# Neighbourhood attention in slots of two units, with scores over row halves of the array

## The chip, the cores and the metric

The kernel runs on one core of one Trainium2 chip. The core has a matrix engine (TensorE, in the profile PE for its matmuls and PEld for its weight loads), a vector engine (VectorE, DVE), a scalar engine (ScalarE, ACT), a general engine (GpSimd, POOL) and a sync engine (SyncE, SP) that mainly issues transfers. Each engine has its own list of instructions, in the order of the program, and waits on semaphores for what the others produce. The metric is the device time of one execution, in microseconds; smaller is better.

## What is computed

The reference is one layer of a bidirectional hybrid encoder over 2048 tokens of width 1024, seen as a grid of 32 rows and 64 columns. One projection yields the inputs of eight attention heads (64 wide) and of four mLSTM heads (128 wide); both branches are gated, concatenated, projected back and added to the input, and a last RMSNorm follows. The change concerns the attention: every token attends to a window of 8 rows and 16 columns.

```python
def neighbourhood_attention(q, k, v, rpb):
    ...
    qg = to_grid(q) * (NA_HEAD_DIM ** -0.5)
    kgrid, vgrid = to_grid(k), to_grid(v)
    ...
    s = jnp.einsum('bhrcd,bhrjkd->bhrcjk', qg, kg).astype(jnp.float32) + bias[None]
    s = jnp.where(col_mask[:, None, :], s, -jnp.inf)
    p = jax.nn.softmax(s.reshape(B, NA_HEADS, rows, GRID_W, kh * GRID_W), axis=-1).reshape(s.shape)
    o = jnp.einsum('bhrcjk,bhrjkd->bhrcd', p, vg)
    ...
def hybrid_mixer(...):
    na_out = neighbourhood_attention(na_q, na_k, na_v, rpb) * jax.nn.silu(na_z)
    ...
    return jnp.concatenate([na_out, ml_out], axis=-1) @ w_out
...
h_res = h_res + gate[:, None, :] * y
return rmsnorm(h_res, final_norm_w).astype(x.dtype)
```

## The kernel before

**Precision.** Large products are made in a one-pass format (F32R) from operands that are split into a high part and a low part, x = hi + lo. A product is the sum of three: hi by hi, hi by lo, lo by hi. The low part is made by ScalarE writing hi and VectorE (or POOL) subtracting it from x.

**Stages.** Phase 1 normalises the input and projects the mLSTM branch. Phase 1b (lines 931 to 962) runs the mLSTM recurrence head by head, and fills the gaps of TensorE with the remaining projections, which `nq_gen` (line 844) yields matmul by matmul: the gates of both branches, then k, then q. The function `pump(n)` (line 917) takes n steps of that stream, and later of the output projections. Phase 2 (line 1209) is attention with the output projection as the filling.

**Keys.** k is kept on chip in four tiles `kk[ct]`, one for two heads (64 rows each). They lie in the memory that the normalised input of token groups 3 and 2 held. The upper half of k goes out to memory and is read back by `kk_jobs` (line 976), sixteen transfers, one at every second step of the recurrence; the lower half is written straight from PSUM (lines 879 to 888). For head j of the pair, a column range of `kk[ct]` holds the high part in 64 rows and the low part in the other 64.

**Queries.** For two units, q is loaded into `qhigh` (the high part twice, in both halves of the rows) and `qlow` (the low part, in the 64 rows of its head, zeros elsewhere, set once by POOL). A matmul with `qhigh` over all 128 rows makes hi by hi plus hi by lo at once, one with `qlow` makes lo by hi. From the fourth load on, `double_q` (line 1267) makes the second copy on VectorE.

**Units and slots.** The grid is cut into 16 patches of 8 by 16 tokens (128 queries). A patch sees 264 to 480 keys. A unit is a patch and two heads, 64 units in all. A slot (line 1531) works on three units at a time:

- `stage_s(n)`: scores, two matmuls a head (lines 1353 and 1354), into a PSUM tile of the pool pS (three buffers); then for each head VectorE adds the bias table and takes the row minimum (line 1359; the scores are negated), ScalarE takes exp with the row sum (line 1360), and the table of a later unit is loaded over the one just used.
- `stage_o(n-2)`: probabilities by v (line 1396), with 64 output columns a head, so each matmul uses half of the array's columns; then VectorE multiplies by the gate (line 1398).
- `stage_t(n-1)`: PE transposes of the normalised probabilities into pT (two buffers, line 1381), evicted by ScalarE (line 1383) into two tiles `pt`.
- `stage_n(n)`: VectorE takes the reciprocal of the sums and normalises (lines 1369 and 1371).
- When a patch is done, its gated output (and the mLSTM half) is split: `mix_high` on ScalarE (line 1406), `mix_low` on VectorE (line 1411). `outproj` (line 1413) is the generator of its 48 projection matmuls (two halves of the output columns, eight blocks of channels, three products each), followed by the addition to x (line 1440), the sum of squares on ScalarE (line 1442), and the scale and the store as later small steps.
- At last, `pump(22)` in the first four slots, all that is left of the q projections in slot 4, and `pump(12)` after that.

In the entry (slots 0 to 5) the stream still holds the last q projections. The dictionary `first` (line 1497) says in which slot which loads and which splits of the output weights (`split_w`, line 1333: ScalarE line 1334, VectorE line 1335) are issued. `load_v`, `load_z` and `load_q(2)` of the first patch stand before slot 0 (lines 1525 to 1527), on POOL's queue.

Phase 2's slots are issued under a manual schedule: the order of the program is the order on each engine.

Of the kernel before, what the change touches and what calls it, by code (L numbers as in the profile page):

```python
# [62 lines left out]
class Kernel:  # L63
# [780 lines left out]
    def nq_gen(self):  # L844
# [10 lines left out]
        for i, s, g in order:  # L855
# [23 lines left out]
            if kind == "k" and g in lower:  # L879

                for j in range(2):
                    rows, other = slice(j * HD, (j + 1) * HD), slice((1 - j) * HD, (2 - j) * HD)
                    cols = slice(j * T + g * GT, j * T + (g + 1) * GT)
                    hv = self.kk[ct][rows, cols]
                    nc.scalar.activation(hv, ps[rows], AF.Identity, bias=bias[rows])
                    nc.vector.scalar_tensor_tensor(self.kk[ct][other, cols], ps[rows], bias[rows], hv.bitcast(F32), ALU.add, ALU.subtract)
                yield
                continue
# [87 lines left out]
    def kk_jobs(self):  # L976

        flat = lambda t: t.rearrange("p a b -> p (a b)")
        self.kk = [flat(t) for g in (3, 2) for t in (self.hhi[g], self.hlo[g])]

        def load(ct, j, hl):
            src = self.d_kna[hl, ct * P + j * HD : ct * P + (j + 1) * HD, T // 2 :]
            row = j * HD if hl == 0 else (1 - j) * HD
            self.nc.sync.dma_start(self.kk[ct][row : row + HD, j * T + T // 2 : (j + 1) * T].bitcast(F32), src)

        return [[((3, 2)[ct // 2], lambda a=(ct, j, hl): load(*a)) for j in range(2) for hl in range(2)] for ct in range(4)]
# [67 lines left out]
    def ml_pass2(self, ml, h):  # L1054
# [11 lines left out]
        def load_z(gi):  # L1066
            while ("mz", h, gi) not in self.zdone:
                self.pump(1)
            if h == MH - 1 and gi == NG - 1:
                t = self.p2.tile([P, 4, P], F32, tag="pt", bufs=2, name="zt_last")  # L1070
# [138 lines left out]
    def phase2(self):  # L1209
# [29 lines left out]
        qhigh = [p.tile([P, 2, 2, P], F32R, name=f"qhigh{i}") for i in range(3)]  # L1239
        qlow = [p.tile([P, 2, 2, P], F32R, name=f"qlow{i}") for i in range(3)]  # L1240
# [14 lines left out]
        def load_q(i):  # L1255
# [3 lines left out]
            hi, lo = qhigh[i % 3], qlow[i % 3]  # L1259
            src = self.d_qna[0, c0 // 2, b].rearrange("(j p) c q -> p j c q", j=2)  # L1260
            for rows in (slice(0, HD), slice(HD, P))[: 2 if i < 3 else 1]:
                (nc.gpsimd if i < 3 else nc.sync).dma_start(hi[rows].bitcast(F32), src)
            for j in range(2):
                js = slice(j * HD, (j + 1) * HD)
                (nc.gpsimd if i < 3 else nc.sync).dma_start(lo[js, j].bitcast(F32), self.d_qna[1, c0 // 2, b, js])

        def double_q(i):
            hi = qhigh[i % 3]
            nc.vector.tensor_copy(hi[HD:], hi[:HD].bitcast(F32))
# [70 lines left out]
        def stage_s(u):  # L1340
            b, ct = units[u]
            pr, pc, nr, nkc, nk, rpc, nch = geo[b]
            at, c = (u // 2) % 3, ct % 2
            pts = []
            sums = few.tile([P, 2], F32, tag="sums", bufs=3, name=f"sums_{u}")
            scores = []
            rs = slice(PR_R0[pr], PR_R0[pr] + nr)
            cs = slice(PC_C0[pc], PC_C0[pc] + nkc)
            for j in range(2):
                ps = pS.tile([P, 512], F32, tag="pS", name=f"pS_{u}_{j}")[:, :nk]  # L1350
                kv = kk[ct][:, j * T : (j + 1) * T].rearrange("p (r c) -> p r c", c=GRID_W)[:, rs, cs]
                o = ps.rearrange("p (r c) -> p r c", c=nkc)
                nc.tensor.matmul(o, qhigh[at][:, j, c, :], kv, start=True, stop=False)  # L1353
                nc.tensor.matmul(o, qlow[at][:, j, c, :], kv, start=False, stop=True)  # L1354
                scores.append(ps)
            for j, ps in enumerate(scores):
# [5 lines left out]
                if u in follows:  # L1362
                    load_tab(follows[u], j)
# [290 lines left out]
```

## Time and profile before

| what | value |
|---|---|
| median of 3 runs | 1388.04 us (1387.38 to 1388.36) |
| the profiled execution, its own time | 1394.31 us |
| its span in the trace | 1392.3 us |
| mean granted clock of TensorE | 0.985 |
| first score of attention (unit 0) | 1014.2 us after the start of the span |
| last value matmuls | 1362.3 us |
| idle TensorE from 1010 to 1030 us | 1.87 us |
| idle TensorE from 1100 to 1363 us | 0 us |

The page of the profile gives busy times for each engine, the chain of work that ended last, and the costliest groups of instructions. A timeline row gives the start in microseconds from the start of the span, the duration, the engine, the line of the kernel, the operation, what is written and read, the shape, and, in brackets, the idle time before it with what ended it. Matmuls are pipelined: a row's duration reaches over the start of the next, so what one costs is the distance from start to start. Rows with x2 or more are several instructions merged.

### The profile page before, as it was taken

How to read it: one execution, taken by the hardware profiler on the slowest of the kernel's cores; microseconds unless marked ns; L12 is line 12 of the kernel's file. 1: busy time of each engine (PE TensorE's matmuls, PEld its weight loads, DVE VectorE, ACT ScalarE, POOL GpSimd, SP SyncE). 2: the span in 40 equal slices, each digit the busy share in tenths (PEclk: the TensorE clock that was granted, in tenths of full speed). 3: DMA queues.
4: the chain of work that ended last, by engine and by line, in shares of the span. 5: the costliest groups of instructions: out<-in, count | busy, mean ns of one | idle time of the engine just before them, and what ended most of it. 6: DMA issues, size and time to landing. Idle time of an engine off the chain costs nothing.

```text
span 1392.3 us, 23366 instructions
## 1 busy us (share of the span) xinstructions
PE 1307.3 (94%) x8076; PEld 1124.4 (81%) x8076; DVE 823.7 (59%) x2497; ACT 528.7 (38%) x1131; POOL 293.7 (21%) x323
## 2 busy tenths in 40 slices
PE   2989999997999899999999999799998999999996
PEld 2989998987877787888878787688876888888885
DVE  6683323211255559156867777877636776777673
ACT  4642334523233323112323313233335555555551
POOL 4453222424101010001212002112402211111121
PEclk9999999999999999999999999999999999999999
DMA  9799439778458685565766888846687896876872
GB/s 317 224 288 226 121 108 230 187 193 192 135 111 216 145 186 159 170 168 146 201 191 204 247 233 226 211 131 185 177 242 232 188 226 162 198 196 169 190 182 61
DMA packets 269723, 263.68 MB, mean 189 GB/s; under 512 B 33482, under 2 KB 230090, under 8 KB 269606
## 3 DMA queue, kind: packets, MB, share of 16 engines
q1 hardware_dynamic: 178062, 186.45, 50.3%
q0 software_dynamic: 21520, 37.73, 11.0%
q10 hardware_dynamic: 70024, 38.02, 9.7%
q8 instruction: 64, 1.05, 0.3%
q14 instruction: 53, 0.43, 0.1%
HBM read 177.57 MB, written 92.72 MB: 194 GB/s over the span
## 4 chain that ended last, share of the span: by engine, by line
PE 51%; DMA 6%; DVE 4%; issue 3%; ACT 1%; POOL 1%; SPq 0%; ACTq 0%; POOLq 0%; DVEq 0%
PE pq L865 17%; PE y L1435 13%; PE pO L1396 4%; PE pT L1381 4%; DMA kv<-d_ck 3%; PE pc L430 2%; PE pc L431 2%; PE pc L429 2%; PE pS L1353 2%; PE px L1091 2%; PE pi L1093 2%; PE pS L1354 2%; PE dc L1039 1%; DMA d_qna<-qst 1%; PE a L1078 1%
## 5 line engine op out<-in xcount | busy, mean ns | idle before, releaser
L865 PE MATMUL pq<-hhi,whi_a 128*128 128x512 f32 x512 | 208.3, 407 | 2.1 <-ACT whi_a L841 1.3
L865 PE MATMUL pq<-hhi,wlo_a 128*128 128x512 f32 x512 | 208.2, 407 | 0.5 <-DVE wlo_a L842 0.5
L865 PE MATMUL pq<-hlo,whi_a 128*128 128x512 f32 x512 | 208.6, 407 | 0.0
L1360 ACT ACTIVATE pbuf<-pbuf,mn 128x480 f32<-128x480 f32 (+5 forms) x128 | 76.3, 597 | 103.3 <-DVE mn L1359 103.1
L865 PEld LDWEIGHTS pq<-hhi,whi_a 128*128 128x128 f32 x512 | 97.4, 190 | 20.1 <-ACT whi_a L841 1.8
L865 PEld LDWEIGHTS pq<-hhi,wlo_a 128*128 128x128 f32 x512 | 97.3, 190 | 17.8 <-DVE wlo_a L842 1.0
L865 PEld LDWEIGHTS pq<-hlo,whi_a 128*128 128x128 f32 x512 | 97.1, 190 | 16.5
L1435 PE MATMUL y<-hhi,whi_a 128*128 128x512 f32 x256 | 86.1, 405 | 3.1 <-ACT hhi L1334 2.8
L1435 PE MATMUL y<-hhi,wlo_a 128*128 128x512 f32 (+1 forms) x272 | 85.1, 386 | 0.2 <-ACT y L1442 0.2
L1359 DVE CUSTOM_DVE_ANT_0 pbuf<-pS,tab 128x480 f32<-128x480 f32 (+5 forms) x128 | 65.1, 541 | 32.6 <-PE pS L1354 24.2
L839 POOL TENSOR_TENSOR wlo_a<-rawq,whi_a 128x1024 fp32r<-128x1024 f32 x20 | 48.1, 2406 | 165.9 <-ACT whi_a L838 124.2
L1115 POOL TENSOR_TENSOR hm<-hm,ck 128x128 f32<-128x128 f32 x64 | 26.3, 412 | 264.1 <-DVE hm L1114 188.8
L429 PE MATMUL pvo<-whi_b,hhi 128*128 128x256 f32 x256 | 74.8, 292 | 5.3 <-DVE stvo L499 5.3
L1096 ACT ACTIVATE num<-px,gtile 128x129 f32<-128x129 f32 x120 | 38.2, 365 | 99.5 <-PE px L1091 83.5
L1023 DVE TENSOR_SCALAR wv<-kv,gtile 128x129 f32<-128x129 f32 x120 | 39.1, 333 | 60.9 <-DMA kv<-d_ck 31.9
L430 PE MATMUL pvo<-wlo_b,hhi 128*128 128x256 f32 x256 | 73.6, 287 | 0.0
L431 PE MATMUL pvo<-whi_b,hlo 128*128 128x256 f32 x256 | 73.5, 287 | 0.0
L714 ACT ACTIVATE dec<-dec,gtile 128x128 f32<-128x128 f32 x128 | 42.1, 392 | 72.3 <-POOL dec L710 63.4
L499 DVE TENSOR_TENSOR stvo<-pvo,brow 128x256 f32<-128x256 f32 x64 | 26.5, 420 | 70.0 <-PE pvo L431 56.2
L464 DVE TENSOR_TENSOR stv<-pv,brow 128x256 f32<-128x256 f32 x32 | 12.4, 421 | 90.2 <-DMA d_vna<-stv 49.1
L1396 PE MATMUL pO<-pt,v 128*64 128x128 f32 (+3 forms) x832 | 60.8, 282 | 0.0
L1381 PE MATMUL pT<-ident,pbuf 128*128 128x128 f32 (+2 forms) x416 | 59.1, 280 | 0.0
(302 smaller groups left out, 3573.0 us busy)
## 6 DMA issues: line engine op xcount, KB each, us to landing
ck<-d_ck SPq DMA_DIRECT2D x64, 384.5 KB
kv<-d_ck SPq DMA_DIRECT2D x120, 128.5 KB
rawq<-in_w_main_dram SPq DMA_DIRECT2D x28, 512.0 KB
raw<-in_w_main_dram SPq DMA_DIRECT2D x20, 512.0 KB
d_ck<-stvo SPq DMA_DIRECT2D x16, 514.0 KB
x<-in_x_dram SPq DMA_DIRECT2D x16, 512.0 KB
wada<-in_w_ada_dram SPq DMA_DIRECT2D x32, 256.0 KB
dec<-d_mneg SPq DMA_DIRECT2D x32, 256.0 KB
```

The costliest lines, as they stand in the source:

```text
L429: nc.tensor.matmul(ps, lhi(k), rhi(k), start=(k == 0), stop=False)
L430: nc.tensor.matmul(ps, lhi(k), rlo(k), start=False, stop=False)
L431: nc.tensor.matmul(ps, llo(k), rhi(k), start=False, stop=(k == KT - 1))
L714: nc.scalar.activation(t[:, d, o, :], t[:, d, o, :], AF.Exp, bias=self.cols["g"][:, d, h, c : c + 1])
L839: nc.gpsimd.tensor_tensor(lo[:, :, cs], raw, hi[:, :, cs].bitcast(F32), ALU.subtract)
L865: nc.tensor.matmul(patch_ps(ps) if patch else ps, w, self.htok(h, g, k, patch), start=(k == 0 and n == 0), stop=(k == KT - 1 and n == 2))
L1023: nc.vector.tensor_scalar(wv, tiles[d, i][:, 128:257], self.cols["w"][:, d, h, c : c + 1], None, ALU.mult)
L1359: nc.vector.tensor_tensor_reduce(pt[:, :nk], ps, tabs[place[u]][j][:, :nk], 1.0, 3e38, ALU.add, ALU.min, mn)
L1360: nc.scalar.activation(pt[:, :nk], pt[:, :nk], AF.Exp, bias=mn, scale=-1.0, accum_out=sums[:, j : j + 1])
L1381: nc.tensor.transpose(ps[:cs, i, :], pts[j][:, i * cs : (i + 1) * cs], self.ident)
L1396: nc.tensor.matmul(po[j * HD : (j + 1) * HD, :], v[:n, h * HD : (h + 1) * HD], pt[j][:n, i, :], start=(i == 0), stop=(i == nch - 1))
L1435: nc.tensor.matmul(y, m[:, k, :], w[k][:, cs], start=(k == 4 and n == 0), stop=(k == 3 and n == 2))
```

## The change

The change rewrites attention's slots and the layout of q and k that its scores read.

- **Layout.** `kk[ct]` holds the high part of both heads in its first T columns and the low part in the next T, with head j in rows 64j to 64j+63. `kk_jobs` has eight transfers of 128 rows where it had sixteen of 64, at the same pace. The lower half's eviction is one ScalarE and one VectorE instruction over 128 rows where it was two and two over 64. q is one tile `qs` of high and low parts, loaded by one transfer; the zeros, the second copy and `double_q` go.
- **Scores.** `scores(pair)` makes for each unit three matmuls a head over the 64 rows of that head, the two heads in turn: high by high, low by high, high by low. pS has four buffers.
- **Slots of two units.** Slot m makes the scores of units 2m and 2m+1, the value matmuls of the two units before (one PSUM tile, one gating instruction), normalises the new pair, and transposes it within the same slot: four times one head's transposes into the single buffer of pT, each followed by its eviction into one of four `pt` tiles and by some steps of the projection stream. The steps of a slot are 44 in the first two and 24 after that.
- **What stands behind the evictions.** The sum of squares (`self.squares`) is no longer issued when the projection ends but behind the next eviction; so are the splits of a finished patch, and the weight splits, one to an eviction. The dictionary `extra` gives their places. The first patch's v, z and q loads are issued in slot 0.

```diff
             if kind == "k" and g in lower:
-                for j in range(2):
-                    rows, other = slice(j * HD, (j + 1) * HD), slice((1 - j) * HD, (2 - j) * HD)
-                    cols = slice(j * T + g * GT, j * T + (g + 1) * GT)
-                    hv = self.kk[ct][rows, cols]
-                    nc.scalar.activation(hv, ps[rows], AF.Identity, bias=bias[rows])
-                    nc.vector.scalar_tensor_tensor(self.kk[ct][other, cols], ps[rows], bias[rows], hv.bitcast(F32), ALU.add, ALU.subtract)
+                hv, lv = (self.kk[ct][:, e * T + g * GT : e * T + (g + 1) * GT] for e in range(2))
+                nc.scalar.activation(hv, ps, AF.Identity, bias=bias)
+                nc.vector.scalar_tensor_tensor(lv, ps, bias, hv.bitcast(F32), ALU.add, ALU.subtract)
...
-        def load(ct, j, hl):
-            src = self.d_kna[hl, ct * P + j * HD : ct * P + (j + 1) * HD, T // 2 :]
...
+        def load(ct, e):
+            src = self.d_kna[e, ct * P : (ct + 1) * P, T // 2 :]
+            self.nc.sync.dma_start(self.kk[ct][:, e * T + T // 2 : (e + 1) * T].bitcast(F32), src)
...
+            (nc.gpsimd if i < 3 else nc.sync).dma_start(qs[i % 3].bitcast(F32), self.d_qna[:, c0 // 2, b].rearrange("e p c q -> p e c q"))
-        def double_q(i):
...
+        def scores(pair):
...
+                for n, (e, f) in enumerate(((0, 0), (1, 0), (0, 1))):
+                    for j, ps in enumerate(made[u]):
+                        js = slice(j * HD, (j + 1) * HD)
+                        o = ps.rearrange("p (r c) -> p r c", c=nkc)
+                        nc.tensor.matmul(o, q[js, e, c, :], keys[f][js], start=(n == 0), stop=(n == 2))
...
+        def turned(u, j):
...
+            for i in range(nch):
+                nc.tensor.transpose(ps[:cs, i, :], U[u][j][:, i * cs : (i + 1) * cs], self.ident)
+            t = p.tile([P, 4, P], F32, tag="pt", bufs=4, name=f"pt_{u}_{j}")
+            nc.scalar.activation(t[:cs, :nch, :], ps[:cs, :nch, :], AF.Copy)
...
-                    nc.scalar.activation(y, x, AF.Square, accum_out=ssq[:, at : at + 1])
+                    square = lambda x=x, y=y, at=at: nc.scalar.activation(y, x, AF.Square, accum_out=ssq[:, at : at + 1])
+                    if end:
+                        square()
+                    else:
+                        self.squares.append(square)
...
-        pS = self.pool(pss, "pS", bufs=3, space=PSUM)
-        pT = self.pool(pss, "pT", bufs=2, space=PSUM)
+        pS = self.pool(pss, "pS", bufs=4, space=PSUM)
+        pT = self.pool(pss, "pT", bufs=1, space=PSUM)
...
+        extra = {
+            (0, -1): [lambda: load_v(b0), lambda: nc.sync.dma_start(zs[1], self.d_mix[b0])],
+            (0, 0): [lambda: load_z(b0), lambda: load_q(2)],
+            (1, 2): [lambda: load_w(4), lambda: load_w(5), lambda: load_w(6), lambda: load_w(7)],
+            (2, 0): [lambda: split_w(4)],
+            (2, 1): [lambda: load_z(b1), lambda: split_w(5)],
+            (2, 2): [lambda: split_w(6), lambda: load_x(b0)],
+            (2, 3): [lambda: split_w(7)],
...
+        def slot(m):
+            new = (2 * m, 2 * m + 1) if 2 * m < NU else ()
+            old = (2 * m - 2, 2 * m - 1) if m else ()
+            if m:
+                load_q(m + 2)
+            if new:
+                scores(new)
+            if old:
+                po = values(old)
+            if new:
+                normalised(new[0])
+            if old:
+                gated(old, po)
+            if new:
+                normalised(new[1])
...
+            fills = [10, 9, 9, 8, 8] if m < 2 else [6, 5, 5, 4, 4]
+            for fn in extra.pop((m, -1), ()):
+                fn()
+            self.pump(fills[0])
+            for n, (u, j) in enumerate([(u, j) for u in new for j in range(2)]):
+                turned(u, j)
+                if n % 2:
+                    step()
+                finish()
+                if n == 1:
+                    if m == 2:
+                        self.pump(max(0, self.left) + 1)
+                        self.owed = 0
+                    mixed(1)
+                if n == 2:
+                    mixed(0)
+                for fn in extra.pop((m, n), ()):
+                    fn()
+                self.pump(fills[n + 1])
```

196 lines of the change are left out of this document (79 added, 117 removed).

## The prediction

> **What bounds the kernel now.** I read the busy shares first, then the chain of waits, then busy time by stretch.
>
> ```profile
> PE 1307.3 (94%) x8076; PEld 1124.4 (81%) x8076; DVE 823.7 (59%) x2497; ACT 528.7 (38%) x1131; POOL 293.7 (21%) x323
> PE 51%; DMA 6%; DVE 4%; issue 3%; ACT 1%; POOL 1%; SPq 0%; ACTq 0%; POOLq 0%; DVEq 0%
> 1030.00:1060.00 30.00, 26.40 (x159) 20.34 (x157) 16.16 (x43) 14.94 (x33) 5.19 (x9) 0.96 0.96 303
> 1100.00:1200.00 100.00, 100.00 (x692) 81.52 (x691) 72.00 (x236) 53.55 (x144) 18.31 (x29) 1.00 0.83 191
> ```
>
> In a stretch the columns are its length, busy PE, PEld, DVE, ACT and POOL, the granted clock, DMA share and GB/s. Attention is bound by TensorE: it never rests from 1100 to 1200 us, while VectorE is 72% and ScalarE 54% busy. So a change there is worth what it takes off or adds to TensorE's own instructions, as long as nothing comes late to them. Only the entry (1030 to 1060 us) has idle TensorE, 3.6 us.
>
> One unit (two heads of a patch) looks like this, first with 384 keys, then the end of one with 480, then a score with 264:
>
> ```profile
> 1200.82 0.34 PE L1353 MATMUL pS<-hhi,qhigh 128*128 128x384 f32 x1
> 1201.00 0.34 PE L1354 MATMUL pS<-hhi,qlow 128*128 128x384 f32 x1
> 1201.62 0.88 PE L1396 MATMUL pO<-pt,v 128*64 128x128 f32 x12
> 1202.43 0.88 PE L1381 MATMUL pT<-ident,pbuf 128*128 128x128 f32 x6
> 1203.06 0.70 PE L1435 MATMUL y<-hhi,whi_a 128*128 128x512 f32 x2
> ...
> 1142.38 0.38 PE L1353 MATMUL pS<-hlo,qhigh 128*128 128x480 f32 x1
> 1142.60 0.38 PE L1354 MATMUL pS<-hlo,qlow 128*128 128x480 f32 x1
> 1142.92 1.09 PE L1396 MATMUL pO<-pt,v 128*64 128x128 f32 x16
> 1143.94 1.09 PE L1381 MATMUL pT<-ident,pbuf 128*128 128x128 f32 x8
> 1144.79 0.70 PE L1435 MATMUL y<-hhi,whi_a 128*128 128x512 f32 x2
> 1145.33 0.39 PE L1435 MATMUL y<-hlo,whi_a 128*128 128x512 f32 x1
> ...
> 1097.49 0.29 PE L1353 MATMUL pS<-hhi,qhigh 128*128 128x264 f32 x1
> 1097.61 0.28 PE L1354 MATMUL pS<-hhi,qlow 128*128 128x264 f32 x1
> ```
>
> Start to start is what an instruction costs. A score takes 0.12 us with 264 keys, 0.18 with 384, 0.22 with 480: 0.46 ns a key. The value stage takes 0.81 us for 12 matmuls and 1.02 for 16, so 0.0525 each and 0.18 fixed: the switch from half-array (128*64) matmuls back to whole ones. The switch into them is 1142.60 to 1142.92 less the 0.22, so 0.10. That is 0.28 a unit, 0.14 a switch. A transpose is 0.105 (0.63 for 6), and the output projection 0.23 (1145.33, less the two before it: 0.27 each, so the step from transposes to projection costs under 0.1).
>
> **The change, part by part.** The forecast adds these terms.
>
> *Scores.* Before, four matmuls a unit over all 128 rows. After, six over 64 rows, alternately rows 0-63 and 64-127, into different PSUM tiles. The patches have 264, 288, 360, 360 keys and 352, 384, 480, 480, each list twice: 5936 keys, by 4 units, by 4 matmuls, by 0.46 ns is 43.7 us now. If the two of a pair run side by side, it is 3/4 of that, 32.8: a gain of 10.9. If they run in turn, it is 6/4, 65.5: a loss of 21.8. Row halves are not in this trace. The nearest rows are the column halves of the value stage. Two such matmuls take 0.105, as one transpose of 128 columns does, and their weight loads end in pairs, as three cuts of one stage show:
>
> ```profile
> 1142.97 0.24 PEld L1396 LDWEIGHTS pO<-pt,v 128*64 128x64 f32 x3
> 1142.97 0.25 PEld L1396 LDWEIGHTS pO<-pt,v 128*64 128x64 f32 x4
> 1142.97 0.35 PEld L1396 LDWEIGHTS pO<-pt,v 128*64 128x64 f32 x5
> ```
>
> The fourth load ends 0.01 after the third, the fifth 0.10 later. So halves of the array load and multiply side by side, and I take -10.9.
>
> The Trainium skill, in "TensorE: Matmul & The Clock Gate" (LDWEIGHTS), lets a load's time go by its columns and not its rows, 128 columns at 1.2 GHz, so a 64-row load would cost a whole one, about 107 ns. By that, with loads in turn, the scores would be the third rival below; the paired ends above speak against it. The page's part on row tiling has matmuls in different row groups run at once, which no row here shows for rows.
>
> *Switches.* Before, two a unit: 128. After, three a pair of units (into row halves, to column halves, back): 96. At 0.14 that is -4.5. The new kinds could cost 0 or double (0 to 0.28 for two of three), so -13 to +4.5; I take -4.5, since all three end one shape and begin another. Transposes now come in four bursts a pair instead of two; a burst inside a run of projections costs nothing extra:
>
> ```profile
> 989.42 0.38 PE L1148 MATMUL ht<-perm,hm 128*128 128x128 f32 x2
> 989.55 0.48 PE L865 MATMUL pq<-hhi,whi_a 128*128 128x512 f32 x1
> 989.87 0.40 PE L865 MATMUL pq<-hlo,whi_a 128*128 128x512 f32 x1
> ```
>
> 0.45 us for two transposes and a 0.23 projection leaves 0.11 each. The projection matmuls are the same in number (24 steps a pair, as 12 twice).
>
> *The new chain inside a slot.* Softmax and transposes of a pair now stand in one slot, where before a unit's transposes came a slot later.
>
> ```profile
> 1206.46 0.56 DVE L1359 CUSTOM_DVE_ANT_0 pbuf<-pS,tab 128x384 f32<-128x384 f32 x1 [0.69 <-PE pS L1354]
> 1206.95 0.08 DVE L1359 DVE_READ_ACCUMULATOR2_ANT mn<- 128x1 f32 x1
> 1208.41 0.17 DVE L1369 RECIPROCAL sums<-sums 128x2 f32<-128x2 f32 x1 [0.48 <-ACT pbuf L1360]
> 1208.61 0.75 DVE L1371 TENSOR_SCALAR pbuf<-pbuf,sums 128x384 f32<-128x384 f32 x2
> 1208.28 0.85 ACT L1383 ACTIVATE pt<-pT 128x384 f32<-128x384 f32 x2
> ```
>
> With 384 keys TensorE reaches the first transpose after six score pairs (1.08), 24 value matmuls (1.26), two switches (0.28) and six projections (1.38): 4.0 us. VectorE begins about 0.7 in (two pairs and a score's 0.34), has four reductions at 0.49, a reciprocal at 0.2 and half of 0.75: 3.2. That leaves 0.8 us, so its items from the slot before may be no later than that. Between transposes stand five or four projections (1.15, 0.92) against the last matmul's tail and an eviction of 0.43, so the single pT buffer holds unless ScalarE is held for half a microsecond. Wait cost: 0 to 10; I take +2, since ScalarE and VectorE have 46% and 28% to spare. The copy that doubled q on VectorE, two of three q transfers on SP's queue and eight of sixteen k transfers go; SP's queue holds no TensorE work but the tables, so 0.
>
> *Entry.* The weight splits become one a transpose.
>
> ```profile
> 1052.11 1.15 ACTq L915 DMA_DIRECT2D d_qna<-qst  x2
> 1053.31 0.63 ACT L1406 ACTIVATE whi_a<-gtile 128x512 fp32r<-128x512 f32 x1 [1.23 <-DVE qst L903]
> 1057.58 1.99 ACT L1334 ACTIVATE hhi<-hlo 128x1024 fp32r<-128x1024 f32 x2
> 1058.66 2.36 DVE L1335 TENSOR_TENSOR hlo<-hlo,hhi 128x1024 fp32r<-128x1024 f32 x2 [0.69 <-ACT hhi L1334]
> 1058.68 0.80 PE L1435 MATMUL y<-hhi,whi_a 128*128 128x512 f32 x1 [2.76 <-ACT hhi L1334]
> ```
>
> In slot 2 the first output projection now follows the last q projection directly, so it waits for the eviction, two stores (1.15) and the split of z (0.63), some 2.5 us that scores and values covered before. Then splits 5, 6 and 7 (1.0 on ScalarE, then 1.2 on VectorE, each behind an eviction) come just ahead of the projections that read them: some 2 us each, 2.5 + 6 = 8.5 against the 3.6 idle in that stretch now: +5, between -4 and +9. The first v, z and q loads go into slot 0, but they stand on POOL's queue:
>
> ```profile
> 994.32 1.46 POOL L1481 MEMSET qlow<- 128x512 f32 x3
> 1002.65 2.00 POOL L1282 DMA_DIRECT2D v<-d_vna  x3
> ```
>
> They wait for nothing of TensorE, and POOL reaches them sooner without the memsets and most of the q issues. Worth 0.
>
> *Phase 1b.* The k evictions of the lower half go from two and two to one and one.
>
> ```profile
> L885 ACT ACTIVATE hhi<-pq,bcol x8: 667/683/685, 866.2 to 920.9; 64x512 fp32r<-64x512 f32 x8
> L886 DVE SCALAR_TENSOR_TENSOR hhi<-pq,bcol,hhi x8: 744/750/755, 868.6 to 921.9; 64x512 fp32r<-64x512 f32 x8
> PE dc L1039 <- DVE wv L1023: 5.5, 6, 2.1
> PE a L1078 <- DMA ck<-d_ck: 4.3, 2, 2.8
> ```
>
> There are 16 of each kind (8 on hhi shown, as many on hlo); 8 go: 6 us of VectorE and 5.5 of ScalarE, in a stretch where TensorE waits 5.5 us for VectorE's wv. Half of that may come back: -3, between -6 and +4. The loss would come from the k transfers, now double in size at the same pace, ahead of ck on SP's queue, where 4.3 us are already waited.
>
> Sum: -10.9 - 4.5 + 2 + 5 - 3 = -11.4. The profiled execution took 1394.3 us (span 1392.3) and becomes 1382.9; the median of the runs shown, 1388.0, is 6.3 lower, and becomes 1376.6. I say **1377**.
>
> **Rivals.** *The row halves run in turn.* Nothing in the trace excludes it. Scores +21.8 in place of -10.9: 1376.6 + 32.7 = 1409. Slower.
>
> *The slot's own chain decides.* One mechanism: VectorE enters the slot late, so the first transpose waits. The break-even is 11.4 over 31 slots, 0.4 us a slot beyond the slack of 0.8. At 0.6 a slot it costs 19 in place of 2: 1394. For it speaks how short the slack is; against it VectorE's spare 28%.
>
> *Only the weight loads go in turn.* Then a pair costs two loads, 2 x 0.105 (a transpose's pace is a bound on its load), 192 pairs at 0.22 for the longest: 41 us, a gain of 2.5 and not 10.9: 1385. Against it: the paired ends.
>
> *Entry and phase 1b come out well.* -4, -6 and no waits: -10.9 - 4.5 - 4 - 6 = -25: 1363.
>
> **Chances.** Forecast 0.56, row halves in turn 0.11, chain 0.13, loads in turn 0.09, all well 0.11. A measurement of this kernel tells about 0.2% from no change, 2.8 us. Faster: 0.56 + 0.11 + 0.04 of loads in turn = 0.71. Same: 0.05 of loads in turn and 0.03 of the chain = 0.08. Slower: 0.11 + 0.10 = 0.21. The range 1361 to 1397 leaves out the row halves in turn and the worst of the chain and of the unknown bounds; the forecast's own is 1366 to 1385.
>
> **What would show it.** Right: scores whose pairs start within 0.02 us of each other, with a pair's pace of 0.46 ns a key; TensorE still without gaps from 1100 us; three gaps of 0.1 to 0.15 a slot around scores and values. Wrong: a score pair at twice that pace (halves in turn) or at 0.22 whatever the keys (loads in turn); TensorE waiting for VectorE's normalised tile at the first transpose, or for ScalarE's eviction at the others, by more than 0.4 us a slot; waits at the entry far from 8 us; more time lost on ck around 870 us.

## The result, and the profile after

| kernel | median | against the kernel before, 95% interval | span in the profile | granted clock |
|---|---|---|---|---|
| before | 1388.2 us (1387.36 to 1393.72, 6 runs) | 1 | 1392.3 us | 0.985 |
| after | 1406.2 us (1403.01 to 1413.21, 6 runs) | 1.0125 [1.0095, 1.0154] | 1404.7 us | 0.979 |

The change makes the kernel 18 us slower; 1377 was forecast, with 1361 to 1397 as range. The two profiled spans lie only 12.4 us apart, since the profiled execution of before lies 6.1 us above the median in the table. The working below goes by the spans.

First the busy shares of the whole changed kernel, then busy time by stretch, of the changed kernel and, in the last two rows, of the kernel before (length, busy PE, PEld, DVE, ACT and POOL, granted clock, DMA share, GB/s):

```profile
PE 1302.4 (93%) x8204; PEld 1110.7 (79%) x8204; DVE 796.2 (57%) x2428; ACT 531.8 (38%) x1123; POOL 286.9 (20%) x311
```

```profile
1010.00:1030.00 20.00, 12.88 (x53) 9.60 (x52) 5.95 (x18) 6.85 (x14) 0.00 (x0) 0.74 0.65 183
...
1060.00:1100.00 40.00, 30.72 (x169) 21.73 (x171) 21.52 (x48) 20.10 (x42) 6.67 (x12) 0.83 0.65 181
1100.00:1200.00 100.00, 97.46 (x742) 76.38 (x738) 66.14 (x219) 55.36 (x143) 18.07 (x30) 1.00 0.79 190
```

```profile
1010.00:1030.00 20.00, 18.13 (x79) 14.36 (x79) 6.36 (x19) 7.33 (x15) 2.57 (x4) 0.93 0.87 230
1060.00:1100.00 40.00, 40.00 (x261) 32.61 (x262) 29.73 (x89) 23.00 (x61) 6.33 (x10) 0.94 0.68 166
```

TensorE's own work got less (1302.4 us busy against 1307.3). What grew is idle time at the entry: 7.1 us from 1010 to 1030, 9.3 us from 1060 to 1100, and in both stretches the granted clock is lower as well (0.74 and 0.83 against 0.93 and 0.94). In the steady part there is a little: 2.5 us in 100, where there was none. TensorE's waits over the whole run name the places (total, times, longest):

```profile
PE pq L865 <- DVE qst L900: 7.1, 1, 7.1
...
PE y L1426 <- ACT hhi L1319: 3.3, 2, 1.8
PE pT L1367 <- DVE pbuf L1359: 3.0, 4, 1.1
PE y L1426 <- ACT whi_a L1397: 2.6, 1, 2.6
...
PE y L1426 <- DVE hlo L1320: 2.4, 5, 0.8
```

Where the difference arises is read from the first score of a slot, which both traces have (a slot of after against two units of before): the first of all, that of slot 6 (unit 12), that of slot 31 (unit 62); before, then after. Only distances within a trace tell something here: at the first matmul of L865, where the stream of projections begins and up to which the kernels do the same, the traces of this document already spread from 547 to 559 us (554.3 before, 556.0 after).

```profile
1014.24 0.30 PE L1353 MATMUL pS<-hhi,qhigh 128*128 128x288 f32 x1
...
1092.63 0.29 PE L1353 MATMUL pS<-hlo,qhigh 128*128 128x264 f32 x1
...
1348.30 0.29 PE L1353 MATMUL pS<-hlo,qhigh 128*128 128x288 f32 x1
```

```profile
1024.78 0.77 PE L1339 MATMUL pS<-hhi,qs 64*128 64x288 f32 x6
...
1109.53 0.64 PE L1339 MATMUL pS<-hlo,qs 64*128 64x264 f32 x6
...
1361.81 0.66 PE L1339 MATMUL pS<-hlo,qs 64*128 64x288 f32 x6
```

The first score is 10.5 us late, slot 6 is 16.9 late. From there to slot 31 the changed kernel takes 252.3 us and the kernel before 255.7: 25 slots win 3.4 us. So the slots do gain, some 0.14 us each, and in these traces the entry is late by five times as much as these 25 slots bring. The 0.14 is from one pair of traces: with the same slots, runs 1, 2 and 3 take 251.6, 254.6 and 250.3 us for this distance, and the old slots of run 4 take 257.5.

**The gap of 7.1 us in slot 0.** The changed kernel around it, queues and engines together:

```profile
998.91 1.38 POOL L1267 DMA_DIRECT2D v<-d_vna  x2
1000.51 18.22 SPq L830 DMA_DIRECT2D rawq<-in_w_main_dram  x2
...
1015.85 1.06 ACT L841 ACTIVATE whi_a<-rawq 128x1024 fp32r<-128x1024 f32 x1 [13.41 <-DMA rawq<-in_w_main_dram]
1016.81 0.67 ACT L899 ACTIVATE qst<-pq,bcol 128x512 fp32r<-128x512 f32 x1
1018.97 0.76 PE L865 MATMUL pq<-hhi,whi_a 128*128 128x512 f32 x1 [7.12 <-DVE qst L900]
```

The same load in the kernel before:

```profile
999.97 10.02 SPq L830 DMA_DIRECT2D rawq<-in_w_main_dram  x2
1007.11 1.06 ACT L841 ACTIVATE whi_a<-rawq 128x1024 fp32r<-128x1024 f32 x1 [5.13 <-DMA rawq<-in_w_main_dram]
```

Read the start of each row: rawq, one of the last 512 KB pieces of the projection weight, is issued at 1000.0 or 1000.5 us in both, and its split on ScalarE starts 7.1 us later before and 15.3 us later after. Behind that split, in ScalarE's order, stands the eviction of q (L899; the trace names its second half on VectorE, L900), and without it TensorE has no PSUM tile for the next q projection. What differs ahead of it is GpSimd: it reached the first v load at 1002.65 before, and at 998.91 after. The queues in the four microseconds from 1002 to 1006, after and then before (packets, MB, share of the 16 DMA engines; q1 is SP's queue with rawq, q0 GpSimd's, q10 ScalarE's):

```profile
q0 software_dynamic: 502, 0.64, 62.3%
q1 hardware_dynamic: 422, 0.22, 27.7%
q10 hardware_dynamic: 141, 0.07, 9.3%
```

```profile
q1 hardware_dynamic: 972, 0.49, 44.0%
q10 hardware_dynamic: 679, 0.34, 28.2%
q0 software_dynamic: 102, 0.24, 22.2%
```

SP's queue moved less than half as much, and ScalarE's a fifth, while GpSimd's moved nearly three times as much. The Trainium skill, in "DMA: Bandwidth & Descriptors" (Queues, rings and completion order), has each DMA engine take the queues that have work in turn, a packet at a time. These rows fit that, 0.22 MB against 0.49 MB in the same time, but they show amounts and not turns.

**A slot in the steady part.** The start of one slot with 384 keys in both units:

```profile
1211.29 0.63 PE L1426 MATMUL y<-hhi,whi_a 128*128 128x512 f32 x2
1211.85 0.80 PE L1339 MATMUL pS<-hlo,qs 64*128 64x384 f32 x6
1212.48 0.70 PE L1339 MATMUL pS<-hhi,qs 64*128 64x384 f32 x6
1213.12 1.53 PE L1382 MATMUL pO<-pt,v 128*64 128x128 f32 x24
1214.58 0.50 PE L1426 MATMUL y<-hlo,whi_a 128*128 128x512 f32 x1
1214.92 0.63 PE L1426 MATMUL y<-hhi,whi_a 128*128 128x512 f32 x2
```

Twelve half-array scores take 1.27 us (1211.85 to 1213.12), where the eight whole ones of two units take 1.60 (twice 0.80 in the rows of before). Six pairs at 0.178 are 1.07; so 0.20 goes to switches inside. The two projections ahead take 0.56 instead of 0.46, the 24 value matmuls 1.46, which is 0.20 above 24 x 0.0525, and the projection behind them 0.34 instead of 0.23. All switches of the slot so come to 0.10 + 0.20 + 0.20 + 0.11 = 0.61 us. In the rows of before one unit's come to 0.09 (0.80 less 4 x 0.178) and 0.18 (0.81 less 12 x 0.0525), and two units' to 0.54.

### The profile page after: what moved, and what is told of

Its sections match the earlier page's. It is cut to its first block, busy times and chain, and to the rows that moved or that the text cites. A ratio compares the mean times of both kernels' runs of the same rounds, so it can differ in the third digit from the quotient of the medians.

```text
span 1404.7 us, 23343 instructions
## 1 busy us (share of the span) xinstructions
PE 1302.4 (93%) x8204; PEld 1110.7 (79%) x8204; DVE 796.2 (57%) x2428; ACT 531.8 (38%) x1123; POOL 286.9 (20%) x311
## 3 DMA queue, kind: packets, MB, share of 16 engines
q0 software_dynamic: 21280, 37.33, 10.9%
## 5 line engine op out<-in xcount | busy, mean ns | idle before, releaser
L865 PE MATMUL pq<-hhi,whi_a 128*128 128x512 f32 x512 | 209.1, 408 | 7.9 <-DVE qst L900 7.1
L865 PE MATMUL pq<-hlo,whi_a 128*128 128x512 f32 x512 | 209.5, 409 | 0.0
L865 PE MATMUL pq<-hhi,wlo_a 128*128 128x512 f32 x512 | 209.0, 408 | 0.0
L865 PEld LDWEIGHTS pq<-hhi,whi_a 128*128 128x128 f32 x512 | 97.8, 191 | 26.0 <-issue 7.7
L865 PEld LDWEIGHTS pq<-hhi,wlo_a 128*128 128x128 f32 x512 | 97.8, 191 | 16.7 <-issue 0.2
L865 PEld LDWEIGHTS pq<-hlo,whi_a 128*128 128x128 f32 x512 | 97.6, 191 | 16.7 <-issue 0.2
L1369 ACT ACTIVATE pt<-pT 96x384 f32<-96x384 f32 (+3 forms) x128 | 66.1, 516 | 92.6 <-PE pT L1367 92.3
L1426 PE MATMUL y<-hhi,whi_a 128*128 128x512 f32 x256 | 92.7, 419 | 7.1 <-ACT hhi L1319 3.3
L1426 PE MATMUL y<-hhi,wlo_a 128*128 128x512 f32 (+1 forms) x272 | 91.1, 397 | 1.1 <-ACT wlo_a L1397 0.8
L1092 ACT ACTIVATE num<-px,gtile 128x129 f32<-128x129 f32 x120 | 38.2, 365 | 104.2 <-PE px L1087 86.2
L1367 PEld LDWEIGHTS pT<-ident,pbuf 128*128 128x128 f32 (+2 forms) x416 | 50.9, 137 | 25.3 <-ACT pt L1369 6.5
L1367 PE MATMUL pT<-ident,pbuf 128*128 128x128 f32 (+2 forms) x416 | 67.6, 276 | 3.3 <-DVE pbuf L1359 3.0
```

The lines of the kernel that those rows point to most:

```text
L865: nc.tensor.matmul(patch_ps(ps) if patch else ps, w, self.htok(h, g, k, patch), start=(k == 0 and n == 0), stop=(k == KT - 1 and n == 2))
L1367: nc.tensor.transpose(ps[:cs, i, :], U[u][j][:, i * cs : (i + 1) * cs], self.ident)
L1369: nc.scalar.activation(t[:cs, :nch, :], ps[:cs, :nch, :], AF.Copy)
L1426: nc.tensor.matmul(y, m[:, k, :], w[k][:, cs], start=(k == 4 and n == 0), stop=(k == 3 and n == 2))
```

## The experiments

Each kernel below is timed against runs of the kernel before on the same chip (medians of before 1387.0 to 1390.3 us). Diffs are against the changed kernel unless said otherwise.

**1. Hold GpSimd until rawq has landed.**

```
             if new:
-                scores(new)
+                scores(new) if m else (scores(new), nc.gpsimd.tensor_copy(held, self.rawq[2][:, 0, 0:1]))
```

> The changed kernel with one thing more: ahead of the first v, z and third q loads GpSimd copies one column of the last projection weight (rawq), so that these loads are issued only when that weight has landed. Theory: the loads that moved forward share the DMA engines with rawq and make it land 15 us after its issue instead of 7; held back, rawq lands again within 8 us, TensorE's 7.1 us gap ahead of the second last q projection goes, and the time falls by 6 to 9 us, to 1397 to 1400. Rival 1: rawq is slow of itself there, lands as late as before and the time stays at 1406. Rival 2: the v chunks, now some 8 us later, take the stall over in front of the first value matmuls: the gap moves to slot 1 and the time stays within 2 us of 1406.

Measured: 1392.67 us, ratio 1.0046 [1.002, 1.0071]: by the ratios 11 us less than the change, somewhat more than the 6 to 9 expected. The split of rawq starts 5.9 us after its issue (993.48 to 999.40). TensorE is busy all through the stretch in which it had idled, at the full clock, and no wait on q is left. GpSimd's copy, behind which the loads go out, and the stretch:

```profile
1006.98 0.19 POOL L1541 COPY held<-rawq 128x1 f32<-128x1 f32 x1 [15.08 <-DMA rawq<-in_w_main_dram]
```

```profile
1010.00:1030.00 20.00, 20.00 (x121) 16.07 (x121) 8.95 (x27) 9.09 (x24) 2.42 (x4) 1.00 1.04 302
```

The v chunks go out at 1007.11 instead of 998.91, in a trace whose projections are 7 us ahead of the change's there (by 8 us already at the first matmul of L865, so that is no effect of the edit), and no matmul waits for them: rival 2 falls with rival 1. The kernel is still slower than before, though.

**2. The weight splits earlier, q's end ahead of the first transpose of slot 2.**

```
-            (1, 2): [lambda: load_w(4), lambda: load_w(5), lambda: load_w(6), lambda: load_w(7)],
-            (2, 0): [lambda: split_w(4)],
-            (2, 1): [lambda: load_z(b1), lambda: split_w(5)],
-            (2, 2): [lambda: split_w(6), lambda: load_x(b0)],
-            (2, 3): [lambda: split_w(7)],
+            (1, 1): [lambda: load_w(4), lambda: load_w(5), lambda: load_w(6), lambda: load_w(7)],
+            (1, 3): [lambda: split_w(4), lambda: split_w(5)],
+            (2, 1): [lambda: load_z(b1), lambda: split_w(6)],
+            (2, 2): [lambda: split_w(7), lambda: load_x(b0)],
...
-            self.pump(fills[0])
+            if m == 2:
+                self.pump(max(0, self.left) + 1)
+                self.owed = 0
+                fills[1:3] = [2, 3]
+            else:
+                self.pump(fills[0])
...
-                if n == 1:
-                    if m == 2:
-                        self.pump(max(0, self.left) + 1)
-                        self.owed = 0
+                if n == (0 if m == 2 else 1):
                     mixed(1)
```

> The changed kernel with the entry into the output projection rearranged: the weights 4 to 7 are loaded one transpose earlier, splits 4 and 5 stand at the end of slot 1, 6 and 7 one transpose earlier than now; the rest of the q projection runs ahead of the first transpose of slot 2 and the z split follows that transpose, so that two transposes stand between the last q eviction and the first long wait. Theory: the waits of slot 2 (2.6 us on the z split, 1.75 and 1.5 us on weight splits, and VectorE's part) fall to 1 to 2 us together: 4 to 6 us off, 1400 to 1402. Rival: the two splits in slot 1 delay the exponentials and reductions of slot 2 by as much, so the wait only moves to the first transpose: 1404 to 1408.

Measured: 1397.06 us, ratio 1.0088 [1.0057, 1.0119], in time what the theory said (5 us off by the ratios, though the interval overlaps that of the change), but not in the way it said. The waits on splits fell, and one wait on the z split grew from 2.6 to 6.1 us. Why is seen in the next run, where it is the same.

**3. Both.** The two diffs together.

> Both of the edits before in one kernel. Theory: two separate stalls, so the gains add: 10 to 15 us off, 1391 to 1396, still a little above the kernel before since the slots themselves gain only 5 to 6 us. Rival: the two are one stall that moves along (what TensorE wins at slot 0 it waits at slot 2): no more than the better of the two alone, 1397 or above.

Measured: 1388.16 us, ratio 1.0012 [0.9989, 1.0035]. The stalls are two and not one: by the ratios 11 and 5 us, and 16 together; against run 1 this run is 4.5 us faster in the mean (twelve runs of each, 95% interval 0.9 to 8.1). The two edits bring the change level with the kernel before. What is left in slot 2 stands in two rows, ScalarE's stores of the last q and TensorE's wait:

```profile
1051.34 4.62 ACTq L912 DMA_DIRECT2D d_qna<-qst  x2
...
1057.06 0.79 PE L1426 MATMUL y<-hhi,whi_a 128*128 128x512 f32 x1 [6.15 <-ACT whi_a L1397]
```

Issuing two stores held ScalarE for 4.62 us (1.15 in the change), and the z split stood behind them.

**4. The mirror: the kernel before with its first v and z loads earlier.** The diff is against the kernel before.

```
                 load_tab(follows.pop(-1 - i), j) if j else load_tab(follows[-1 - i], j)
+            if i == 0:
+                load_v(b0)
+                load_z(b0)
...
-        load_v(b0)
-        load_z(b0)
         load_q(2)
```

> The mirror: the kernel before, with nothing changed but GpSimd's order: the first three v chunks and the first z are issued between the first and the second unit's q loads, some 3.5 us earlier, inside the time in which rawq is under way. Theory: rawq then lands late in the kernel before as well, by 3 to 8 us, and TensorE gets a gap before the last q projections: 2 to 7 us slower, 1390 to 1395. Rival: the order of these loads is not what held rawq: 1388 as before.

Measured: 1394.09 us, ratio 1.0038 [1.0013, 1.0062]: slower by 2 to 9 us, as expected, with nothing changed but the order of one queue. Its rows:

```profile
1011.11 1.06 ACT L841 ACTIVATE whi_a<-rawq 128x1024 fp32r<-128x1024 f32 x1 [9.06 <-DMA rawq<-in_w_main_dram]
...
1014.23 0.47 PE L865 MATMUL pq<-hhi,whi_a 128*128 128x512 f32 x1 [2.81 <-DVE qst L903]
```

rawq, issued at 1000.00, now starts its split after 11.1 us instead of 7.1, and the gap ahead of q that the change has opens here too, 2.8 us long. Together with the first run this settles the larger half of the loss.

**5. The entry put in order.** On top of the third kernel: the last two q stores through SP's queue; in slot 2 both units' normalisation, then the rest of q, then the values; the z split behind the q eviction and ahead of the first transpose; splits 6, 7 at transposes 0 and 1 of slot 2, split 0 at its last, 1 to 3 in slot 3.

```
         while late:
-            nc.scalar.dma_start(*late.pop(0))
+            nc.sync.dma_start(*late.pop(0))
...
+            if m == 2:
+                normalised(new[0])
+                normalised(new[1])
+                self.pump(max(0, self.left) + 1)
+                self.owed = 0
             if old:
                 po = values(old)
...
+            if m == 2:
+                mixed(1)
+                gated(old, po)
```

> The third kernel carried on. In it the z split stood behind the two stores of the last q eviction on ScalarE, whose issue took 4.6 us, and TensorE waited 6.2 us for it. Here these stores go through SP's queue; in slot 2 the rest of the q projection runs ahead of the value matmuls, and the z split directly behind the q eviction, so that values and a transpose cover it; splits 6, 7, 0, 1, 2, 3 each stand one or two transposes earlier. Theory: the entry then costs 2 to 3 us instead of 13: 8 to 10 us off the third kernel, 1378 to 1381, below the kernel before by the 7 us that the slots themselves gain. Rival: the wait only passes to the first transpose of slot 2 or to the weight loads of the second half, and it stays within 4 us of the third kernel: 1384 to 1388.

Measured: 1379.13 us, ratio 0.9936 [0.9913, 0.9959]: 9 us faster than the kernel before, 26 us by the ratios faster than the change, with the slots as the change has them. In slot 2 the stretch from the end of the q projection (its last matmul starts at 1050.19) to the first output projection now runs without a wait:

```profile
1050.52 1.53 PE L1382 MATMUL pO<-pt,v 96*64 96x128 f32 x24
1051.98 0.54 PE L1367 MATMUL pT<-ident,pbuf 128*120 128x128 f32 x3
1052.28 0.48 PE L1426 MATMUL y<-hhi,whi_a 128*128 128x512 f32 x1
```

Values and a transpose (1.8 us) cover what ScalarE does between them.

**6. Six projection steps held back as a cover for later patches; the z split ahead of the squares.**

```
-                fills[1:3] = [2, 3]
+                fills[1:5] = [1, 2, 2, 2]
...
-                finish()
                 if n == 1 and m != 2:
                     mixed(1)
+                finish()
```

> The same with six projection steps fewer in slot 2 (7 instead of 13), so that each later patch's projection still has six steps of the patch before it to run when its z split is made, and with that split ahead of the squares on ScalarE. Theory: the waits at a patch's start (1.2 us at the second patch in the third kernel, some 0.3 us at others) go, 1 to 3 us, against 1.4 us more of projections left at the end: within 2 us of the run with the entry alone, 1377 to 1381. Rival: the waits at the starts of patches are larger in sum than the gaps show: 4 us or more off.

Measured: 1384.31 us, ratio 0.9972 [0.9946, 0.9997], outside the 1377 to 1381 of the theory. The intervals of the ratios overlap with run 5's, but both were timed on one chip, and there the twelve runs average 1383.3 us against 1379.6, so a loss is likelier than none. The trace says where to look: from 1100 us on VectorE waits 7.3 us for bias tables (4.5 in run 5), and TensorE waits 7.9 us at first transposes from 1000 us on (3.2 in run 5). Run 12 takes that up.

**7 and 9. The half-array scores alone, in one-unit slots.** The kernel before with `qs`, the k evictions, the transfers of k and q and the score loop of the change. In run 7 the copy of rawq was written ahead of the loads, outside the slots, and was put behind them on GpSimd's queue; in run 9 copy and loads stand in the first slot.

> The kernel before with the row-half scores alone (the q and k layout with them, one unit a slot, two pT buffers, squares and splits as before), and GpSimd held until rawq has landed. Theory: the paired scores gain their 10.9 us, but a third switch of 0.19 us comes into every unit (12.2 us for 64), so nothing is left: 1386 to 1391, and the score's start after a projection is late by 0.2 us in every unit. By the prediction's own price of 0.14 us for a switch it is 1.9 us faster, 1386. Rival: the new switch costs nothing beyond the old two: 1377.

Measured in run 7: 1396.46 us, ratio 1.0066 [1.0043, 1.0089], against 1386 to 1391. Its GpSimd rows show why this was no test of the scores:

```profile
1003.38 1.37 POOL L1267 DMA_DIRECT2D v<-d_vna  x2
...
1025.69 0.18 POOL L1509 COPY held<-rawq 128x1 f32<-128x1 f32 x1 [15.99 <-DMA rawq<-in_w_main_dram]
```

rawq was issued at 1004.97, 1.6 us behind the v loads, the copy came last, and TensorE waited 5.0 us for q: the stall of the change in a third kernel, by accident. Hence run 9.

> The row-half scores alone in the kernel before once more, now with the copy of rawq and the first v, z and third q loads inside the first slot, so that GpSimd cannot reach the loads ahead of the copy as it did in the run before (there v was issued 1.6 us ahead of rawq and TensorE waited 5.0 us). Theory: without that stall what the pairs gain and what the switch into row halves costs in every unit nearly cancel (+1.3 us for 64 units): 1386 to 1392, ratio 0.999 to 1.003. By 0.14 us for a switch it is 1386. Rival: the rows themselves lose 8 us, the stall was not the reason: 1395 or more.

Measured in run 9: 1392.54 us, ratio 1.0007 [0.9987, 1.0027]: nothing, as the theory said, and 8 us of run 7 are gone with the stall. The price of 0.14 us a switch would give 0.9986, at the very edge of the interval, so the rows have to decide. One unit with 384 keys:

```profile
1198.61 0.39 PE L1420 MATMUL y<-hlo,whi_a 128*128 128x512 f32 x1
1198.93 0.80 PE L1340 MATMUL pS<-hhi,qs 64*128 64x384 f32 x6
1199.66 0.88 PE L1381 MATMUL pO<-pt,v 128*64 128x128 f32 x12
```

Its scores take 0.73 us instead of 0.80, and start 0.32 after the projection instead of 0.23: 0.07 won, 0.09 given back. So the pairs are worth something only where two units share the switch.

**8 and 11. The order of the score matmuls.** Run 8 gives a unit's three matmuls on rows 0 to 63 first and then its three on rows 64 to 127; run 11 gives a slot's six and then its six.

```
-                for n, (e, f) in enumerate(((0, 0), (1, 0), (0, 1))):
-                    for j, ps in enumerate(made[u]):
+                for j, ps in enumerate(made[u]):
+                    for n, (e, f) in enumerate(((0, 0), (1, 0), (0, 1))):
```

> The changed kernel with the order of the score matmuls alone changed: of each unit the three on rows 0 to 63 first, then the three on rows 64 to 127, so that neighbours in the queue share a row half. Theory: only neighbours on different halves run side by side; of the 12 in a slot that is left for three pairs (the third and fourth, sixth and seventh, ninth and tenth), so a slot's scores take 9 single matmuls' time instead of 6: +16 us, 1422. Rival 1: no overlap at all without the alternation: +33 us, 1439. Rival 2: the order doesn't matter, the queue finds its pairs: 1406.

Measured in run 8: 1404.11 us in a single run, which fits rival 2; the rows settle it. A slot with 480 keys has the same pace in the changed kernel (first) and in this one: 0.77 us from one unit's scores to the other's.

```profile
1253.68 0.93 PE L1339 MATMUL pS<-hhi,qs 64*128 64x480 f32 x6
1254.45 0.83 PE L1339 MATMUL pS<-hlo,qs 64*128 64x480 f32 x6
```

```profile
1251.07 0.94 PE L1339 MATMUL pS<-hhi,qs 64*128 64x480 f32 x6
1251.84 0.83 PE L1339 MATMUL pS<-hlo,qs 64*128 64x480 f32 x6
```

> The changed kernel with a slot's twelve score matmuls in two blocks of six: all on rows 0 to 63 first, then all on rows 64 to 127. Theory: with blocks of three the second half's stream started with the first, so TensorE looks at least three instructions ahead; if it looks six ahead the pairs still start together and the time stays at 1404 to 1407. Rival: the look-ahead is four: of six, the third or fourth onward overlap, some 2 to 3 matmuls a slot are alone, 0.35 to 0.5 us a slot, 11 to 16 us more: 1416 to 1422.

Measured in run 11: 1420.16 us in a single run, inside the rival's 1416 to 1422. A slot with 384 keys:

```profile
1215.89 0.91 PE L1341 MATMUL pS<-hlo,qs 64*128 64x384 f32 x4
1216.53 0.34 PE L1341 MATMUL pS<-hhi,qs 64*128 64x384 f32 x1
...
1217.62 0.55 PE L1384 MATMUL pO<-pt,v 128*64 128x128 f32 x6
```

The queue holds three on hlo, three on hhi (both rows 0 to 63), then three on hlo and three on hhi for rows 64 to 127. Four on hlo start before the first on hhi: the seventh of the queue has overtaken the fourth. But it starts only with the third: one by one, the starts are 1215.89, 1216.17 and 1216.35 for the first three, 1216.36 for the seventh and 1216.53 for the fourth. So the second half begins 0.47 us after the first, and the twelve take 1.73 us instead of 1.27.

**10. More projections ahead of the first transpose.** On run 5:

```
-            fills = [10, 9, 9, 8, 8] if m < 2 else [6, 5, 5, 4, 4]
+            fills = [10, 9, 9, 8, 8] if m < 2 else [8, 4, 4, 4, 4]
```

> The kernel of the entry run with the projections of a slot dealt out as 8, 4, 4, 4, 4 around the four transposes instead of 6, 5, 5, 4, 4, which gives the softmax 0.46 us more before the first transpose. Theory: the waits at first transposes (1.2, 0.7, 0.9 and 0.6 us in the entry run's trace) go, 2 to 4 us off: 1375 to 1378. Rival: the shorter stretches of 4 between the other transposes make TensorE wait for the eviction of the single pT buffer: the same or slower, 1379 to 1385.

Measured: 1386.06 us, ratio 0.9959 [0.9931, 0.9988]: not the 1375 to 1378 of the theory but nearer the rival, although the interval overlaps that of run 5. From 1000 us on, waits for the normalised tile fall from 3.2 to 1.4 us against run 5, and those for the pT eviction rise from 0.4 to 1.6, those for the squares from 1.4 to 2.9: the slack was moved and not made.

**12. Three pairs of bias tables.** On run 5, with q in two tiles to make the room:

```
-        tabs = [[p.tile([P, 480], F32, name=f"tab{i}{j}") for j in range(2)] for i in range(2)]
+        tabs = [[p.tile([P, 480], F32, name=f"tab{i}{j}") for j in range(2)] for i in range(3)]
...
-            place.append(place[same[0]] if same else (1 - place[u - 1] if u else 0))
+            place.append(place[same[0]] if same else min(range(3), key=lambda q: user.get(q, q - 3)))
```

VectorE's waits for tables from 1100 to 1370 us, before and then after:

```profile
DVE pbuf L1359 <- DMA tab<-d_t: 6.3, 8, 2.4
```

```profile
DVE pbuf L1347 <- DMA tab<-d_t: 3.1, 5, 1.1
```

> The kernel of the entry run with three pairs of bias tables instead of two (room made by keeping q in two tiles, loaded behind the scores). In the traces with two-unit slots VectorE waits for a table in 2 to 8 slots (1.3 to 4.8 us), and TensorE's waits on the normalised tile at first transposes go with it (3.0 us in the changed kernel, 3.2 us in the entry run). Theory: in the kernel before the same waits (6.3 us, 8 times) lay under the slot that then stood between softmax and transposes; now they reach TensorE. A table loaded a unit earlier removes them: VectorE's wait for tables under 1 us, TensorE's waits at first transposes under 1 us from 1100 us on, 2 to 4 us off: 1375 to 1378, ratio 0.990 to 0.992. Rival: VectorE itself is late at these slots, whatever the tables do: the waits at first transposes stay at 3 us and the time within 1 us of the entry run, ratio 0.993 to 0.994.

Measured: 1377.44 us, ratio 0.9927 [0.9901, 0.9952], a ratio between what the theory (to 0.992) and the rival (from 0.993) gave. In this trace VectorE waits for no table in that stretch, and TensorE's only wait from 1100 us on is this one, for the squares:

```profile
PE y L1426 <- ACT y L1433: 1.4, 3, 0.6
```

From slot 6 to slot 31 it takes 249.3 us, 6.4 less than before, where the change won 3.4. By the times alone run 12 can't be told from run 5. By the trace, in which both waits are gone together, the table waits are what stood behind the first transposes; the tables and the two tiles for q were not tried apart. This is the fastest of the kernels, 10 us below before.

## Why the prediction was wrong

By its own steps, against the profiled spans. The step that failed is the one on the first v, z and q loads; the switches are the next largest error.

- **Scores, -10.9.** Right. Pairs run side by side at 0.46 ns a key: three pairs of 384 keys and one switch take 0.63 us (1211.85 to 1212.48), 3 x 0.178 and 0.10, and the two of the first pair start 0.003 us apart. That the row halves run in turn, and that only the weight loads do, are both out.
- **Switches, -4.5.** Wrong in size. The sum counted 128 against 96 at one price of 0.14. Three switches of a slot cost 0.61 us, 0.20 each, and the four they replace 0.54; what was priced by the old kinds costs half as much again in the new. Run 12, almost free of waits, bounds what is left: -6.4 us in 25 slots is -8.1 for 32, where scores and switches were to give -15.4. The waits for the squares (1.4 us, 1.8 for 32 slots) are part of that difference; the other 5.5 us are this term, gone to about +1. By the rows of one slot (0.61 against 0.54) it is +2.2 for 32. Run 9 shows the same from the other side.
- **The slot's own chain, +2.** The wait is real and of the size taken: 3.0 us at first transposes, far from the 0.4 us a slot at which that rival decides. What makes VectorE late is not its spare time but the bias tables: before, 6.3 us of waiting for them lay under the slot between softmax and transposes; in the shorter chain VectorE's 3.1 us of it come out as TensorE's 3.0. In run 12 both are gone. That the size fits is luck: the sum took it from the engines' spare time and had no term for the tables.
- **The first v, z and q loads, "Worth 0".** This is the step that failed, by some 10 us of the 24 between forecast and measurement. It asked what the loads wait for and who waits for them, and not what they run beside. The trace of before had a sign that this stretch has no slack: of the 1.87 us in which TensorE idles from 1010 to 1030, 1.3 are a wait for the split of the next rawq (L841), while the prediction named only 1030 to 1060 as idle. Coming 3.7 us sooner, they shared the DMA engines with rawq, rawq landed 8 us later, and 7.1 us of TensorE with a stretch at 0.74 of the clock were lost. Run 1 takes it away (11 us), run 4 puts it into the kernel before.
- **Entry in slot 2, +5 of -4 to +9.** Right in mechanism, with the splits and the z split as named: waits of 2.6, 3.3 and 2.4 us are 8.3, against the 8.5 that were worked out. Set against the 3.6 us of before that is +4.7; but the clock fell with it (0.83 from 1060 to 1100 us), which the sum had no term for: from slot 0 to slot 6 the change takes 84.8 us against 78.4, 6.4 more, though its slots are shorter. In run 5 the same stretch takes 72.5 us, with nothing changed there but the order of the work and the queue of the last q stores.
- **Phase 1b, -3.** About -1. TensorE's wait on ck fell from 4.3 to 0.5 us and one of 5.3 us on ScalarE (L1092) came in its place, for a reason that no run looked for. The q projection at 1003 us is 0.5 us late, but the first matmul of that stream was already 1.7 us late.

In sum: 10.5 us up to the first score and 6.4 us to slot 6 against the +5, -3.4 us in 25 slots against some -10.5 (25/32 of -13.4), and -1.1 from slot 31 to the end: 12.4 us. The term that had been set to nothing is the largest miss, but it does not turn the sign alone: without it, in run 1, the kernel is still 0.5% slower than before (0.2 to 0.7), and with 5 us less at slot 2, in run 3, it is level. The "What would show it" was answered by pairs that started together, and by waits at the entry far from 8 us.

What stays open: by which rule ScalarE's stores take 1.15 us to issue in one order and 4.62 in another, and whether run 10, which dealt the projections out differently, loses against run 5 or only seems to.

## What to carry to other kernels

A load that nobody waits for can still cost time by when it runs: before moving one earlier, look at what else is in flight then, and who waits for that. A new shape of matmul has to pay for the switches at both ends: here six pairs between them won something and three won nothing. When a buffered stage is shortened, look for waits that the longer one hid (here a table load), since they come out on the engine that sets the end.

## What the hardware showed unexpectedly

- TensorE does not keep the order of its queue between row halves. In run 8 the fourth matmul of a unit starts 0.01 us after the first, in run 11 the seventh starts ahead of the fourth and together with the third. The Trainium skill, in "TensorE: Matmul & The Clock Gate" (Part 3: Packing small matmuls), has matmuls start and end strictly in queue order, and a reorder window 64 deep that pulls weight loads ahead. The rows of run 11 differ on the first point, since a matmul started ahead of three that stood before it in the queue; of the window they show a reach of four places.
- A 512 KB load on SP's queue took 15 instead of 7 us, from issue to use, beside GpSimd's loads, 11 in the mirror and 5.9 with these loads held back (run 1).
- Two stores that ScalarE issues in 1.15 us in one order of the work took 4.62 us in another, and everything behind them in ScalarE's order waited.
